# mLSTM sample states spread over the chunks of the last head, with their sum in another PSUM pool

## The chip, the cores and the metric

The kernel runs on one core of one Trainium2 chip. The metric is the device time of one execution in microseconds, the median of several runs.

## The reference

One layer of a hybrid decoder, over a prompt of 1,024 tokens and 8 samples of 4 tokens that share all weights: a SwiGLU feed-forward block, a mixer, a second SwiGLU block, and a gated per-layer embedding. The mixer projects the normalised tokens once and runs an S5 branch and an mLSTM branch. The change lies in the mLSTM branch:

```python
scores = jnp.einsum('bhtd,bhsd->bhts', qc, kc) * w
num = (jnp.einsum('bhts,bhsd->bhtd', scores, vc)
       + a[..., None] * jnp.einsum('bhtk,bhkv->bhtv', qc, C))
nq = jnp.sum(scores, axis=-1) + a * jnp.einsum('bhtk,bhk->bht', qc, n)
h = num / jnp.maximum(jnp.abs(nq), jnp.exp(-m_t))[..., None]
C_new = decay[..., None, None] * C + jnp.einsum('bhs,bhsk,bhsv->bhkv', wk, kc, vc)
n_new = decay[..., None] * n + jnp.einsum('bhs,bhsk->bhk', wk, kc)
```

The prompt starts from empty states and passes through 8 chunks of 128 tokens. Each of the 8 samples is one chunk of 4 tokens, and starts from given states: per sample and head a matrix C of 256 x 256 and a vector n of 256, which are read, used, updated and written. With 4 heads that is 32 matrices of 256 KB in and as many out. The output of both goes, after a norm by head and a gate `sigmoid(o)`, into the projection `w_m_up`.

## The kernel before

All 1,056 tokens are held with features on the partitions, in three column blocks of 384, 384 and 288 (`CH`). A product of the projections is made of three matmuls with operands split in a high and a low part (`mm3`, lines 115 to 117). The stages are in program order: feed-forward, gates, S5, conv and q/k, then for each head `head_proj` and `head_scan`, then `samples`, the output gate (`proj_tanh` with the name og), the S5 output (`s5_out`: glu, s5u), the join, feed-forward two, embedding, output.

The kernel is written in a framework that keeps a simulated timeline of the engines, and issues an instruction where that timeline has room for it. So the order on each engine isn't the program's: long products without dependences, such as og's 8 x 3 units of 24 matmuls, fill the places where TensorE would wait for a scan. The order is fixed when the kernel is built; on the chip each engine takes its instructions in that order and waits on semaphores. Buffers come from pools: 34 long tiles in SBUF ("slots"), which hold the q, k, v of a head, other tensors of the mixer, and the tiles of C; and two PSUM pools of four banks each, `pm` (tag "mm", for projections like og) and `pv` (tag "aux", for the scan and all small products).

`head_scan` (from line 1181) handles a head chunk by chunk: scores `s` (L1199), the transposed keys `kt` (L1202), weights from a row that is loaded for each chunk (L1196), the weighted scores split in `ps` (L99), their product with the values in `num`, the state's part (L1221), the state update `kv`, and `head_out`, whose transposes (`hT`, L1177) come one chunk later. After the last chunk the head's final state is stored (L1236, L1237).

`samples` is made of two parts. The first prepares: loads, transposes of n and of the keys (`nT` L1271, `ksT` L1278), the scores of all samples and heads at once (`sS`, L1286), from them `Pb` inside the tile `smA` (L1292), and K, V in split form. The second, the inner function `states`, is called after the scan of head 3. It makes the new n (`nn` L1317, added on VectorE at L1321 and L1322, transposed in `nnT` L1325 and stored), then one PSUM bank `snum` for the outputs of all samples: first the product with `Pb` (L1330), then for each of the 8 samples b and each pair of heads hh a tile `c0_b hh` of two matrices:

```python
for i in range(2):
    nc.sync.dma_start(ct[:, i, :, 0:256], ...)
v.tensor_copy(ct[:, :, :, 256:258], nz[...])
```

that is a load from SP (L1343) and a copy of the n columns on VectorE (L1344). Eight matmuls of 258 columns add the tile's part to `snum` (L1348); two matmuls a head make the key-value product `skv` (L1354), VectorE updates the matrices in place (L1356, 0.7 us each), and ScalarE's queue stores them (L1357). At the end `head_out` norms `snum`, transposes it (`hT_smp`) and stores it.

In the run order before, head 3's setup of the samples is called ahead of its scan, and `states()` behind it:

```python
if h == 3:
    states = self.samples()
self.head_scan(h, *qkv)
```

Of the kernel before, what the change touches and what calls it, by code (L numbers as in the profile page):

```python
# [7 lines left out]
F32 = mybir.dt.float32  # L8
# [7 lines left out]
P = 128  # L16
# [19 lines left out]
class Kernel:  # L36
# [1141 lines left out]
            return ps, self.hT[i % 2][:, :, :n]  # L1178
        return transposed

    def head_scan(self, h, q, k, vt):
        nc, v = self.nc, self.nc.vector
        gm = self.gain["g_mhead"]
        Cp = None

        def out(transposed, c):
            ps, hT = transposed()
            for kk in range(2):
                nc.scalar.activation(hT[:, kk], ps[:, kk], AF.Copy, scale=gm[:, 2 * h + kk:2 * h + kk + 1])
            nc.sync.dma_start(self.d_hm[2 * h:2 * h + 2, :, c * P:(c + 1) * P].rearrange("k p t -> p k t"), hT)  # L1190

        for c in range(8):
            nm, sl = f"{h}_{c}", slice(c * P, (c + 1) * P)
            z, wk, em = (self.cols[:, c, i, h:h + 1] for i in range(3))
            bc = self.bc[(8 * h + c) % 4]
            nc.sync.dma_start(bc.rearrange("p q t -> p (q t)"), self.d_row[h, c].rearrange("q t -> (q t)").unsqueeze(0).to_broadcast([P, 256]))  # L1196
            s = self.pv.tile([P, 512], F32, tag="aux", name=f"s{nm}")[:, :P]
            for kk in range(2):
                nc.tensor.matmul(s, k[kk][:, sl], q[kk][:, sl], start=kk == 0, stop=kk == 1)  # L1199
            kt = self.pv.tile([P, 512], F32, tag="aux", name=f"kt{nm}")[:, :256]  # L1200
            for kk in range(2):
                nc.tensor.transpose(kt[:, kk * P:(kk + 1) * P], k[kk][:, sl], self.ident)  # L1202
            kh, kl = (self.kw[:, c % 2, 256 * i:256 * i + 256] for i in range(2))
            nc.scalar.activation(kh, kt, AF.Copy, scale=wk)
            v.scalar_tensor_tensor(kl, kt, wk, kh.bitcast(F32), op0=ALU.mult, op1=ALU.subtract)
            vc = [x[:, c % 4] for x in vt[c // 4]]
            qp = self.pt.tile([P, 384], F32, tag="ss", name=f"qp{nm}")
            p, qa = qp[:, 256:], qp[:, :256].rearrange("p (k t) -> p k t", k=2)
            p2 = self.pt.tile([P, 384], F32R, tag="sq", name=f"ps{nm}")
            ph, pl = p2[:, :P], p2[:, P:2 * P]  # L1210
            v.tensor_tensor(p, bc[:, 0], self.mneg, ALU.add)
            nc.scalar.activation(p, p, AF.Exp, bias=z)
            v.scalar_tensor_tensor(p, s, 1.0 / 64, p, op0=ALU.mult, op1=ALU.mult)
            num = self.pv.tile([P, 512], F32, tag="aux", name=f"num{nm}")[:, :258]
            self.split(p, ph, pl)
            self.mm3(num, (ph, pl), *vc, True, c == 0)
            if c:
                for kk in range(2):
                    v.scalar_tensor_tensor(qa[:, kk], q[kk][:, sl], 1.0 / 32, bc[:, 1], op0=ALU.mult, op1=ALU.mult)
                for kk in range(2):  # L1220
                    nc.tensor.matmul(num, qa[:, kk], Cp[:, kk], start=False, stop=kk == 1)  # L1221
            Cn = self.C_[(8 * h + c) % 2]
            for kk in range(2):
                kv = self.pv.tile([P, 512], F32, tag="aux", name=f"kv{nm}_{kk}")[:, :258]
                ks = slice(kk * P, (kk + 1) * P)
                self.mm3(kv, (kh[:, ks], kl[:, ks]), *vc, True, True)
                if c:
                    v.scalar_tensor_tensor(Cn[:, kk], Cp[:, kk], self.decb[:, 16 * h + c:16 * h + c + 1], kv, op0=ALU.mult, op1=ALU.add)
                else:
                    v.tensor_copy(Cn[:, kk], kv)  # L1230
            Cp = Cn
            if c:
                out(transposed, c - 1)
            transposed = self.head_out(num, em, P, nm)
        out(transposed, 7)
        nc.sync.dma_start(self.outs[4][0, 0, h].rearrange("(k p) x -> p k x", p=P), Cp[:, :, 0:256])  # L1236
        nc.sync.dma_start(self.outs[5][0, 0, h].rearrange("(k p) -> p k", p=P), Cp[:, :, 256])  # L1237
# [12 lines left out]
    def samples(self):  # L1250
# [56 lines left out]
        def states():  # L1307
# [18 lines left out]
            no = self.pt.tile([P, 384], F32, tag="h", name="no")[:32, :256]  # L1326
            v.tensor_copy(no, ps)
            nc.sync.dma_start(self.outs[11][0].rearrange("b h k -> (b h) k"), no)
            num = self.pv.tile([P, 512], F32, tag="aux", name="snum")[:, :258]
            nc.tensor.matmul(num, Pb, self.vs, start=True, stop=False)  # L1330
            for b in range(8):
                bs = slice(4 * b, 4 * b + 4)
                qb = qm[b % 2]
                if b > 1:
                    v.memset(qb[:, :, 4 * b - 8:4 * b - 4], 0.0)
                v.tensor_tensor(qb[:, :, bs].rearrange("p (h k) t -> p h k t", k=2), self.qs[:, :, bs].rearrange("p (h k) t -> p h k t", k=2),
                                asb[:, :, bs].unsqueeze(2).to_broadcast([P, 4, 2, 4]), ALU.mult)
                km = kms[b % 2]
                v.tensor_scalar(km, K[:96, :NP].bitcast(F32).rearrange("p (h x) -> p h x", h=4), self.bmask[:96, b:b + 1], None, op0=ALU.mult)
                for hh in range(2):  # L1340
                    ct = self.px.tile([P, XW], F32, tag="s", name=f"c0_{b}{hh}")[:, :1032].rearrange("p (h k x) -> p h k x", h=2, k=2)
                    for i in range(2):
                        nc.sync.dma_start(ct[:, i, :, 0:256], a["state_mlstm_c"][0, b, 2 * hh + i].rearrange("(k p) x -> p k x", p=P))  # L1343
                    v.tensor_copy(ct[:, :, :, 256:258], nz[:, 4 * b + 2 * hh:4 * b + 2 * hh + 2])  # L1344
                    for kk in range(2):
                        for i in range(2):
                            h = 2 * hh + i
                            nc.tensor.matmul(num[32 * h:32 * h + 32], qb[:, 2 * h + kk], ct[:, i, kk],  # L1348
                                             start=False, stop=b == 7 and kk == 1)
                    for i in range(2):  # L1350
                        h = 2 * hh + i
                        kv = self.pv.tile([P, 512], F32, tag="aux", name=f"skv{b}_{h}").rearrange("p (k x) -> p k x", k=2)
                        for kk in range(2):
                            nc.tensor.matmul(kv[:, kk], km[:, h, kk * P:(kk + 1) * P], V[:96, 256 * h:256 * h + 256], start=True, stop=True)  # L1354
                        cc = ct[:, i, :, 0:256]
                        v.scalar_tensor_tensor(cc, cc, self.decb[:, 16 * h + 8 + b:16 * h + 9 + b], kv, op0=ALU.mult, op1=ALU.add)  # L1356
                        nc.scalar.dma_start(self.outs[10][0, b, h].rearrange("(k p) x -> p k x", p=P), cc)  # L1357
# [167 lines left out]
    def run(self):  # L1525
# [22 lines left out]
        self.scan_setup()  # L1548
        for h in range(4):
            qkv = self.head_proj(xm, sm, w_in, h)  # L1550
            if h == 3:
                states = self.samples()
            self.head_scan(h, *qkv)
        states()
        self.proj_tanh(xm, rb, w_in[:, 3584:4608], self.d_to, "og")
        self.s5_out_load()
        self.s5_out()
# [37 lines left out]
```

## Time and profile before

| | |
|---|---|
| median of 3 runs | 2270.72 us (2268.5 to 2270.73) |
| profiled execution, its own time | 2271.5 us |
| its span, first to last instruction | 2269.8 us |
| mean granted clock of TensorE | 0.994 of full speed |
| TensorE (PE) busy | 2232.9 us, 98%, 15,712 matmuls |
| VectorE (DVE) busy | 1379.9 us, 61% |
| ScalarE (ACT), GpSimd (POOL) busy | 821.7 us, 36%; 501.7 us, 22% |
| DMA | 240.47 MB, 106 GB/s mean |
| chain that ended last | PE 88%, DVE 5%, DMA 4% |

The chain that ended last is followed back from the last instruction to what released each piece; 88% of it is TensorE. A timeline row gives start, duration and, in brackets, the idle time before it with what ended that. Durations of matmuls that follow one another overlap, so their cost is the distance from start to start. A window row gives for a stretch the busy time of each engine and the granted clock as a share of 2.4 GHz.

### The profile page before, as it was taken

Reading aid. Unit: us, or ns where it says so; the run is one execution under the profiler, and the core shown is the slowest. Engines: PE = TensorE matmul, PEld = TensorE weight load, DVE = VectorE, ACT = ScalarE, POOL = GpSimd, SP = SyncE. Lnnn points to the kernel's source line nnn. Section 1 sums busy time; section 2 is a strip of 40 time slices with the busy share of each in tenths; the row PEclk is TensorE's granted clock in tenths of the full one; section 3 lists DMA queues with packets and bytes.
Section 4 is the critical chain, followed back from the end, with each engine's and each line's share of the span. In section 5 each row is a group of like instructions: output and inputs, shape, how many; then the busy total and the mean of one; then the engine's idle time right before and its main releaser. Section 6 shows DMA issues by size and latency. Waiting matters only on the chain.

```text
span 2269.8 us, 39784 instructions
## 1 busy us (share of the span) xinstructions
PE 2232.9 (98%) x15712; PEld 2194.9 (97%) x15712; DVE 1379.9 (61%) x3190; ACT 821.7 (36%) x1552; POOL 501.7 (22%) x528
## 2 busy tenths in 40 slices
PE   7999999999999999999999999999999999999999
PEld 6999999999999999999999889999999999999998
DVE  5854556336768857769686477545665556523754
ACT  6433333114334433444344233224433333311543
POOL 1476763000001000000000000003477666000000
PEclk9999999999999999999999999999999999999999
DMA  5223237223344542222223587342122233711201
GB/s 189 78 68 94 76 95 246 74 69 111 88 126 132 139 122 64 55 64 54 61 63 113 154 275 262 121 152 76 62 80 74 75 95 95 262 64 56 60 20 77
DMA packets 286146, 240.47 MB, mean 106 GB/s; under 512 B 28748, under 2 KB 263212, under 8 KB 285960
## 3 DMA queue, kind: packets, MB, share of 16 engines
q1 hardware_dynamic: 266720, 216.34, 31.0%
q10 hardware_dynamic: 19240, 21.59, 2.8%
q8 instruction: 123, 2.02, 0.4%
q14 instruction: 63, 0.52, 0.1%
HBM read 168.04 MB, written 67.35 MB: 104 GB/s over the span
## 4 chain that ended last, share of the span: by engine, by line
PE 88%; DVE 5%; DMA 4%; issue 1%; SPq 1%; ACT 1%; POOL 0%; ACTq 0%; DVEq 0%
PE mm_qk L115 3%; PE mm_qk L116 3%; PE mm_qk L117 3%; PE mm_f1d L117 2%; PE mm_f1d L115 2%; PE mm_f1d L116 2%; PE mm_f2d L115 2%; PE mm_f2d L116 2%; PE mm_f2d L117 2%; PE mma_f2u L191 2%; PE mmd_f2u L191 2%; PE mmc_f2u L191 2%; PE mmc_f2g L191 2%; PE mmd_f2g L191 2%; PE mma_f2g L191 2%; PE mmc_f1g L191 2%
## 5 line engine op out<-in xcount | busy, mean ns | idle before, releaser
L115 PE MATMUL mm_qk<-n2h,wh_qk 128*128 128x384 f32 (+1 forms) x384 | 126.0, 328 | 0.0
L116 PE MATMUL mm_qk<-n2l,wh_qk 128*128 128x384 f32 (+1 forms) x384 | 125.4, 327 | 0.0
L117 PE MATMUL mm_qk<-n2h,wl_qk 128*128 128x384 f32 (+1 forms) x384 | 125.2, 326 | 0.0
L115 PE MATMUL mm_f1d<-f1hh,wh_f1d 128*128 128x384 f32 (+1 forms) x384 | 122.8, 324 | 1.8 <-DVE x_f L565 1.8
L115 PE MATMUL mm_f2d<-f2hh,wh_f2d 128*128 128x384 f32 (+1 forms) x384 | 123.5, 326 | 1.0 <-ACT f2hh L98 1.0
L117 PE MATMUL mm_f2d<-f2hh,wl_f2d 128*128 128x384 f32 (+1 forms) x384 | 123.7, 323 | 0.0
L116 PE MATMUL mm_f1d<-f1hl,wh_f1d 128*128 128x384 f32 (+1 forms) x384 | 123.7, 323 | 0.0
L117 PE MATMUL mm_f1d<-f1hh,wl_f1d 128*128 128x384 f32 (+1 forms) x384 | 123.7, 323 | 0.0
L116 PE MATMUL mm_f2d<-f2hl,wh_f2d 128*128 128x384 f32 (+1 forms) x384 | 123.6, 323 | 0.0
L1166 POOL TENSOR_TENSOR cy<-cs,mhalf 128x1 f32<-128x1 f32 x32 | 20.2, 632 | 442.2 <-DVE cs L1165 419.2
L429 POOL TENSOR_TENSOR rc_n<-nv_n,mhalf 128x3 f32<-128x3 f32 x9 | 8.9, 984 | 444.0 <-DVE nv_n L425 407.6
L565 DVE SCALAR_TENSOR_TENSOR x_f<-mm_f2d,x_f 128x384 f32<-128x384 f32 (+1 forms) x72 | 37.2, 521 | 94.9 <-PE mm_f2d L117 92.8
L565 DVE SCALAR_TENSOR_TENSOR x_f<-mm_f1d,x_f 128x384 f32<-128x384 f32 (+1 forms) x72 | 36.9, 521 | 93.3 <-PE mm_f1d L117 90.6
L1108 DVE SCALAR_TENSOR_TENSOR cv<-raw,vecs,cv 128x384 f32<-128x384 f32 (+1 forms) x144 | 84.8, 589 | 7.3 <-ACT cv L1106 6.0
L115 PEld LDWEIGHTS mm_f1d<-f1hh,wh_f1d 128*128 128x128 f32 x384 | 71.9, 188 | 2.6 <-DVE x_f L565 2.5
L115 PEld LDWEIGHTS mm_f2d<-f2hh,wh_f2d 128*128 128x128 f32 x384 | 71.9, 188 | 1.8 <-ACT f2hh L98 1.2
L116 PEld LDWEIGHTS mm_qk<-n2l,wh_qk 128*128 128x128 f32 x384 | 72.3, 188 | 0.1
L115 PEld LDWEIGHTS mm_qk<-n2h,wh_qk 128*128 128x128 f32 x384 | 72.3, 188 | 0.0
L117 PEld LDWEIGHTS mm_qk<-n2h,wl_qk 128*128 128x128 f32 x384 | 72.2, 188 | 0.1
L116 PEld LDWEIGHTS mm_f1d<-f1hl,wh_f1d 128*128 128x128 f32 x384 | 72.2, 188 | 0.0
L117 PEld LDWEIGHTS mm_f2d<-f2hh,wl_f2d 128*128 128x128 f32 x384 | 72.1, 188 | 0.1
L116 PEld LDWEIGHTS mm_f2d<-f2hl,wh_f2d 128*128 128x128 f32 x384 | 72.1, 188 | 0.0
(761 smaller groups left out, 7370.7 us busy)
## 6 DMA issues: line engine op xcount, KB each, us to landing
d_f1h<-f1h SPq DMA_DIRECT2D x16, 528.0 KB
f1hl<-d_f1h SPq DMA_DIRECT2D x16, 528.0 KB
x_f<-d_xs SPq DMA_DIRECT2D x16, 528.0 KB
d_f2h<-f2h SPq DMA_DIRECT2D x16, 528.0 KB
f2hl<-d_f2h SPq DMA_DIRECT2D x16, 528.0 KB
wr_qk<-in_w_in_dram SPq DMA_DIRECT2D x16, 512.0 KB
c<-in_state_mlstm_c_dram SPq DMA_DIRECT2D x32, 256.0 KB
out_dram<-c ACTq DMA_DIRECT2D x32, 256.0 KB
```

Source lines behind the costliest of these rows:

```text
L115: mm(ps, wh, xh, start=start, stop=False)
L116: mm(ps, wh, xl, start=False, stop=False)
L117: mm(ps, wl, xh, start=False, stop=stop)
L191: nc.tensor.matmul(ps, w[:, wq, i], f[q][:, xq, cs], start=start and i == j == 0, stop=i == n - 1 and j == 2, skip_group_check=not start)
L429: nc.gpsimd.tensor_tensor(r, ms, self.mhalf[:, :nt], ALU.pow)
L565: v.scalar_tensor_tensor(xs, ps, 0.5, xs, op0=ALU.mult, op1=ALU.add)
L1108: v.scalar_tensor_tensor(acc, raw[:, o + i:o + i + wd], self.cw[:, i, T:T + 1], acc, op0=ALU.mult, op1=ALU.add)
L1166: nc.gpsimd.tensor_tensor(y, ss, self.mhalf[:n, 0:1], ALU.pow)
```

## The change

`head_scan` takes a function `then` and calls it after each chunk. `states` becomes a generator: a `yield` stands ahead of each sample of its loop. The run order scans heads 0 to 2 as before; then it calls the setup and makes the generator, and scans head 3 with `then` drawing one step. So after chunk 0 the part up to the first product into `snum` is written, after chunk c the sample c - 1, and after the scan sample 7 with the closing part. And `snum` takes its bank from `pm`, where og's units have theirs.

```diff
-    def head_scan(self, h, q, k, vt):
+    def head_scan(self, h, q, k, vt, then=lambda: None):
...
             transposed = self.head_out(num, em, P, nm)
+            then()
         out(transposed, 7)
...
-            num = self.pv.tile([P, 512], F32, tag="aux", name="snum")[:, :258]
+            num = self.pm.tile([P, 512], F32, tag="mm", name="snum")[:, :258]
             nc.tensor.matmul(num, Pb, self.vs, start=True, stop=False)
             for b in range(8):
+                yield
                 bs = slice(4 * b, 4 * b + 4)
...
         for h in range(4):
             qkv = self.head_proj(xm, sm, w_in, h)
-            if h == 3:
-                states = self.samples()
-            self.head_scan(h, *qkv)
-        states()
+            if h < 3:
+                self.head_scan(h, *qkv)
+        states = self.samples()()
+        self.head_scan(3, *qkv, lambda: next(states))
+        for _ in states:
+            pass
```

Lines of `samples` move down by one or two: the first product into `snum` is L1331, the load L1345, the copy L1346, the update L1358.

On TensorE, at the start of head 3's scan, where the setup's scores `sS` have just been made, the order changes as follows (`s_0` and `kt_0` are chunk 0's scores and transposed keys, `mm_og_0` is og's first unit, `smA` holds Pb):

```order
-L1286 MATMUL sS<-mlE 32x32 x8
+L1272 MATMUL nT<-ident,nin 128x32 x2
+L1279 MATMUL ksT_13462<-ident,mlE 32x128 x4
+L1279 MATMUL ksT_13463<-ident,mlE 32x128 x4
+L1287 MATMUL sS<-mlE 32x32 x8
+L1199 MATMUL s_0_13529<-q_0_12714,k_0_12716 128x128
+L1199 MATMUL s_0_13529<-q_1_12715,k_1_12717 128x128
+L1202 MATMUL kt_0_13532<-ident,k_0_12716 128x128
+L1202 MATMUL kt_0_13532<-ident,k_1_12717 128x128
+L1331 MATMUL snum<-mlE,smA 128x258
 L115 MATMUL mm_og_0_14343<-n2h_5775,wh_og_14339 128x384
```

Before, og's first product stood right behind `sS`; now chunk 0's `s` and `kt` and the first product into `snum` stand between them.

On VectorE, at chunk 3 of head 3, the order before was (`qp_3` are the weighted scores, `ps_3` their split, `kw` the weighted keys, `cd_2` a column of chunk 2's `head_out`):

```order
L1213 SCALAR_TENSOR_TENSOR qp_3_13695<-s_3_13687,qp_3_13695 128x128
L1165 TENSOR_SCALAR cs_2_13672<-cs_2_13672 128x1
L99 TENSOR_TENSOR ps_3_13696<-qp_3_13695,ps_3_13696 128x128
L1167 TENSOR_TENSOR cd_2_13670<-cy_2_13673 128x1
L1168 TENSOR_TENSOR cd_2_13670<-cd_2_13670,cs_2_13672 128x1
L1205 SCALAR_TENSOR_TENSOR kw<-kt_3_13690,cols,kw 128x256
```

At the same place the order of the change is:

```order
L1358 SCALAR_TENSOR_TENSOR c_11_13775<-c_11_13775,decb,skv_3_13788 128x2x256
L1341 TENSOR_SCALAR sm_13496<-smK,bmask 96x1024
L1213 SCALAR_TENSOR_TENSOR qp_3_13802<-s_3_13794,qp_3_13802 128x128
L1346 COPY c_20_13852<-smA 128x4x2
L1205 SCALAR_TENSOR_TENSOR kw<-kt_3_13797,cols,kw 128x256
L99 TENSOR_TENSOR ps_3_13803<-qp_3_13802,ps_3_13803 128x128
```

The update of tile c_11 and the copy into tile c_20 now stand among chunk 3's work, the copy ahead of its `kw` and `ps`. The tile c_20 takes the buffer of tile c_10.

## Rows read from the trace of the kernel before

**Rows 1.** Windows of 10 us: busy of PE, PEld, DVE, ACT, POOL (count), PEclk, DMA share, GB/s.
```profile
1290.00:1300.00 10.00, 6.74 (x48) 6.45 (x47) 1.29 (x5) 2.21 (x4) 0.00 (x0) 0.96 0.81 140
...
1350.00:1360.00 10.00, 9.26 (x61) 8.91 (x60) 10.00 (x20) 4.22 (x10) 0.00 (x0) 1.00 0.62 201
```

**Rows 2.** Waits of TensorE, 1195 to 1365: us in total, times, longest us.
```profile
PE nnT L1325 <- DVE smA L1322: 3.3, 1, 3.3
PE hT_smp L1177 <- DVE mlC L1172: 0.7, 1, 0.7
```

**Rows 3.** Timeline of TensorE around nnT: start us, us, engine, line, operation.
```profile
1296.39 0.34 PE L117 MATMUL mm_og<-n2h,wl_og 128*128 128x384 f32 x1
1299.99 0.58 PE L1325 MATMUL nnT<-ident,smA 128*32 128x128 f32 x2 [3.26 <-DVE smA L1322]
```

**Rows 4.** Windows behind three waits of TensorE, columns as in rows 1.
```profile
1299.20:1306.00 6.80, 6.01 (x32) 2.98 (x34) 3.60 (x9) 0.45 (x1) 0.00 (x0) 0.50 0.41 126
...
657.50:667.70 10.20, 8.45 (x41) 8.05 (x42) 5.25 (x19) 1.50 (x2) 0.48 (x1) 0.50 0.41 95
...
561.00:567.00 6.00, 6.00 (x37) 6.00 (x37) 6.00 (x16) 4.53 (x9) 0.00 (x0) 1.00 0.96 311
```

**Rows 5.** Chain that ended last, ahead of nnT: start us, us, what.
```profile
1288.33 0.56 SPq L1237
1288.94 10.56 DMA c<-in_state_mlstm_c_dram
1299.59 0.13 DVE c L1344
```

**Rows 6.** Chain that ended last: og, and a c tile's round trip.
```profile
1277.62 0.13 PE mm_og L116
...
1282.36 5.50 DMA c<-in_state_mlstm_c_dram
...
1307.11 0.37 PE mm_og L115
1307.48 0.18 PE mm_og L116
1307.66 0.23 PE skv L1354 x2
...
1308.07 0.17 PE mm_og L115
...
1312.27 0.76 DVE c L1356
1313.06 4.30 DMA out_dram<-c
1317.43 0.37 SPq L1343
1317.85 3.92 DMA c<-in_state_mlstm_c_dram
```

**Rows 7.** Timeline of VectorE: Pb (smA, L1292) with its neighbour, and an og evacuation.
```profile
1205.67 1.22 DVE L99 TENSOR_TENSOR wl_og<-wr_og,wh_og 128x1024 fp32r<-128x1024 f32 x1
1206.81 0.78 DVE L1292 SCALAR_TENSOR_TENSOR smA<-sS,smA 32x32 f32<-32x32 f32 x4
...
1291.90 0.56 DVE L628 TENSOR_TENSOR t_og<-mm_og,rb_n 128x384 f32<-128x384 f32 x1 [1.53 <-PE mm_og L117]
```

**Rows 8.** Timeline of TensorE, start of head 3's scan.
```profile
1203.83 0.44 PE L115 MATMUL mm_og<-n2h,wh_og 128*128 128x384 f32 x1
...
1207.60 0.61 PE L1199 MATMUL s<-q,k 128*128 128x128 f32 x4
...
1208.18 0.42 PE L115 MATMUL mm_og<-n2h,wh_og 128*128 128x384 f32 x1
```

**Rows 9.** Timeline of TensorE: two other waits.
```profile
560.76 0.40 PE L115 MATMUL mm_f1d<-f1hh,wh_f1d 128*128 128x288 f32 x1 [1.50 <-DVE x_f L565]
...
659.25 0.48 PE L787 MATMUL h0T<-ident,s5w 128*128 128x128 f32 x1 [3.82 <-DMA s5w<-in_state_s_re_dram]
```

## The prediction

> **What bounds the kernel now.** I read the table of busy times first: TensorE is busy for nearly the whole span, so time is won or lost only where it stands still or runs at its lower clock. The 10 us windows around the change come second. There TensorE is full, except that it does 6.74 us in 1290 to 1300 and 9.26 us in 1350 to 1360 [rows 1]. The list of its waits over 1195 to 1365 names two: 3.3 us for nnT, 0.7 us for hT_smp [rows 2]. In the timeline the last og product ends at 1296.73 and nnT starts at 1299.99 [rows 3]. The granted clock then stands at 0.50, which is 1.2 GHz, from 1299.20 to 1306.00, with TensorE busy 6.01 us of it [rows 4].
>
> Why nnT waits is read from the chain that ended last. VectorE takes its work in order, and the add into smA that nnT needs stands behind a copy into a c tile whose load took 10.56 us; that load was issued right behind the scan's last store (L1237) [rows 5]. So a state load that is late for a later tile holds back the first tile's sum.
>
> **What the old place costs.** The wait is 3.26 us. Work of 6.01 us at half clock would be 3.0 us at full clock: 3.0 lost. The wait before hT_smp is 0.74. Together 7.0 us can be won, no more, since TensorE has no other wait there.
>
> **The change, part by part.**
>
> *Instructions.* Matmuls, loads, updates and stores of the samples stay the same in number and shape. TensorE's work does not change, only its neighbours do. Counted along the two orders from sS to the end of glu, TensorE changes between og-like and full fp32 products 87 times before and 79 times now. The first og product after snum products takes 0.37, a later one 0.17 [rows 6]; eight changes fewer, half of them into og, are 4 x 0.20 = **-0.8**.
>
> *Removed.* nn, its add and nnT now stand in the second chunk's og products, ahead of any late load; the scan's last store now stands behind all c loads on SP. The 3.26, the 3.0 of clock, and the 0.74 (snum ends well before glu) go: **-7.0**.
>
> *Added at the head.* snum's first product moves to just behind sS and chunk 0's s and kt, ahead of every og product. It needs Pb, the masked score block. VectorE finishes Pb only at 1206.81 + 0.78 = 1207.59, since the og weight split (1.22 us) stands ahead of it [rows 7], and its order up to Pb is unchanged. TensorE follows sS with og at 1203.83; s and kt take 1208.18 - 1207.60 = 0.58 [rows 8]. So TensorE reaches snum at 1203.83 + 0.58 = 1204.41 and waits 1207.59 - 1204.41 = **+3.2**. Behind snum in TensorE's order stands all of og, which hid Pb before; now that cover is gone. The bounds are 0, if VectorE gets Pb done sooner, and 3.3.
>
> *Clock after it.* No row shows this wait, so I take its neighbours. The 3.26 wait was followed by 6.80 us at 0.50, a 3.82 wait by 10.20 us at 0.50 (8.45 busy) and a 1.50 wait by full clock [rows 3, 4, 9]. 3.2 lies beside 3.26, so the drop is likely: **+3.0**, bounds 0 and 4.2 (half of 8.45).
>
> *The c tiles.* Before, the 16 tiles of c were spread over some eleven buffers and came at the end. Now, beside the live tiles of head 3, two buffers are free, a third after chunk 3. So each of the tiles from c_10 to c_41 waits for its predecessor's round trip: update 0.76, store 4.30, SP 0.37, load 3.92, which with what lies between is 1317.85 + 3.92 - 1312.27 = 9.5; with a load of 5.50 it is 11.1 [rows 6]. What TensorE has to do between, counted along its order (og at 0.175, the mean of its 0.17 and 0.18, or 0.13; two skv 0.23 [rows 6]), is 10.2 us ahead of c_10, 9.4 ahead of c_11, 9.5 ahead of c_21, 12 to 13 from c_40 on. For c_20 it is worst: VectorE's copy into c_20 stands ahead of chunk 3's kw and ps, so the chunk's num waits for the load too. From tile 10's last product to that num lie 37 og of 384 columns (6.5), 10 of 288 (1.3), four skv (0.46), s and kt (0.6): 8.9. c_31 (9.7) and c_41 (10.4) stand so as well. Against 9.5 the stalls are 0.6 and a little, against 11.1 they run to 2.2, 1.7, 1.6, 1.4, 0.9 and 0.7, sum 8.5; but one stall lengthens the gap of the next, so I take half of it as the upper end, then add a clock drop: 0 to 7. Value: **+2.0**, nearer the first end, since transfers are now spread over the whole scan, where the rows come from a crowded stretch.
>
> *og's bank.* snum holds one of og's four banks for the whole scan. A unit of 24 products takes 24 x 0.175 = 4.2 us, its evacuation on VectorE 0.56 [rows 7]; with three banks two units (8.4 us) hide it: **0**. If VectorE were held by a c copy for over 8 us the bank would matter; this is inside the c tiles' upper end.
>
> *Tail.* The y5 load of the last quarter now waits for a buffer of chunk 7; a late one costs at most a load, 5.5 [rows 6]. I take **0**, since og still follows.
>
> *Sum.* -0.8 - 7.0 + 3.2 + 3.0 + 2.0 = +0.4. The profiled execution is 2271.5, its span 2269.8; the sum makes it 2271.9. The median is 2270.72, so on its scale **2271.1 us**: no change. One stall at the scan's end is traded for one at its head.
>
> **A rule against the change.** The rows show a repeated two-buffer round trip with 0.6 to 2.2 us between need and arrival [rows 6]. The Trainium skill, "Perfetto Trace Analysis", section "Optimization Strategy", says that the same gap repeating on the engine that should be saturated can mean too little SBUF or PSUM for the next tile. By it the gap would return with each batch; that is rival B. The Trainium skill, "TensorE: Matmul & The Clock Gate", section "HAM oscillation", describes a loop whose wait for data re-throttles the clock in every round, so that the work behind starts slow; by it rival B would pay the clock each time. Here the 1.50 wait kept full clock [rows 4, 9], which speaks against that for short stalls.
>
> **The rivals.**
> *A, faster.* The head's wait leaves the clock at full and the c tiles come in time: -0.8 - 7.0 + 3.2 = -4.6, so 2266.1. For it: 1.50 left the clock alone. Against: 3.26 and 3.82 did not. Should Pb also come 1.2 earlier (the og split issued behind it), 2264.9. Chance 0.24.
> *B, slower.* The two-buffer round trip sets the pace of batches 1 to 4. It decides when store plus load take over about 10 us in the new place. With loads of 5.50 the stalls are 4.3, and if two of them run together past 3 us the clock adds 3.0: +7.3 in place of +2.0, so 2276.4; with a second such drop 2279.4. For it: the 10.56 us load [rows 5]. Against: that load shared the queues with the scatter store, now moved. Chance 0.26.
> *C, nothing new.* Of the forecast's terms only sizes vary. 0.50. That the change does nothing is excluded by the order: nnT and snum do move.
>
> **How the numbers follow.** About 0.2% (4.5 us) is what a measurement of this kernel can tell from no change: faster lies below 2266.2, slower above 2275.3. A falls just below the first, B above the second. C's own range is 2267 to 2275: the c tiles 0 to 5, the clock 2 to 4. The range of 8 in 10 takes in most of A and half of B: 2265.3 to 2277.5. Chances: faster 0.23, same 0.52, slower 0.25.
>
> **What would show it.** Right: in TensorE's waits, nnT and hT_smp gone; snum's first product waiting some 3 us for smA from VectorE at about 1204; the granted clock at 0.5 for some microseconds behind it and at 1.0 around 1300; waits of 0 to 2 us ahead of num of chunks 3 to 5 or snum, released by VectorE's c copy or the c load. Wrong: no wait at snum's first product, or og running ahead of it (A and less); full clock after the wait (A); stalls that repeat with each batch beyond 2 us (B); a wait of og for its bank; glu waiting for y5.

## The result, and the profile after

The change is slower: 2285.62 us median of 4 runs (2283.55 to 2286.87), against 2270.72 before. The ratio is 1.0065 [1.0053, 1.0077]. Forecast were 2271.1 us and no change, with a range up to 2277.5; the result lies 8 us above it. The profiled execution of the change has a span of 2285.1, which is 15.3 more than before's 2269.8.

Windows of before, cut at three places in TensorE's order: the end of `sS`, the last of glu and cvT (the transposes of the conv branch), the end of the up projection `mm_mu`. Columns as in [rows 1]:

```profile
1203.90:1375.70 171.80, 167.80 (x1106) 154.19 (x1106) 111.46 (x320) 68.18 (x148) 4.86 (x9) 0.98 0.62 195
1375.70:1514.60 138.90, 138.90 (x864) 138.90 (x863) 82.00 (x154) 34.26 (x61) 0.00 (x0) 1.00 0.48 163
```

The same two stages after:

```profile
1205.50:1382.40 176.90, 171.62 (x1104) 155.49 (x1105) 108.55 (x315) 69.33 (x148) 4.84 (x9) 0.99 0.61 181
1382.40:1529.80 147.40, 141.87 (x866) 140.59 (x865) 84.43 (x159) 34.10 (x61) 0.00 (x0) 0.99 0.48 163
```

The first stage, head 3's scan with the samples, takes 5.1 us longer. The second, s5u and the join, takes 8.5 us longer, though the change names nothing in it: there TensorE had no idle time before, and has 5.5 now. The start took 1.6 more; nothing in it is changed, and the end of `sS` lay between 1201.9 and 1207.4 over the kernels of this study, but for one that moves work from ahead of it to behind it. So totals are read beside their stages below.

TensorE's waits of 1195 to 1480 after, columns as in [rows 2]:

```profile
PE mm_s5u L115 <- DVE g L1410: 2.8, 2, 1.8
PE mm_mu L115 <- DVE g L1410: 2.6, 1, 2.6
PE snum L1331 <- DVE smA L1293: 2.3, 1, 2.3
PE skv L1356 <- ACT mlC L1189: 1.9, 1, 1.9
PE hT L1177 <- DVE mlC L1172: 0.7, 1, 0.7
PE s L1199 <- DVE smA L1274: 0.2, 1, 0.2
```

nnT and hT_smp [rows 2] are gone, as forecast. The wait at snum's first product is there, as forecast. The others are new. TensorE's timeline at the head, columns as in [rows 3], where [rows 8] had og right behind `sS`:

```profile
1205.12 0.35 PE L1287 MATMUL sS<-mlE 128*32 128x32 f32 x16
1205.64 0.71 PE L1199 MATMUL s<-q,k 128*128 128x128 f32 x4 [0.17 <-DVE smA L1274]
1206.48 0.41 PE L1202 MATMUL kt<-ident,k 128*128 128x128 f32 x2
1209.22 0.70 PE L1331 MATMUL snum<-mlE,smA 128*128 128x258 f32 x2 [2.33 <-DVE smA L1293]
```

Windows after: the two spells at half clock (the second follows the 1.83 us wait before s5u), the place of nnT in [rows 1], and what follows the waits for skv and mu:

```profile
1210.23:1213.65 3.42, 3.42 (x13) 3.42 (x12) 3.24 (x11) 2.62 (x8) 0.00 (x0) 0.50 1.10 341
1418.45:1421.86 3.41, 3.41 (x13) 3.41 (x12) 1.90 (x6) 0.99 (x2) 0.00 (x0) 0.50 1.02 406
1290.00:1300.00 10.00, 10.00 (x65) 9.10 (x64) 3.81 (x18) 2.45 (x8) 0.00 (x0) 1.00 0.73 244
...
1351.97:1360.00 8.03, 8.03 (x53) 8.00 (x54) 4.54 (x10) 2.11 (x3) 0.00 (x0) 1.00 0.86 276
...
1440.40:1448.00 7.60, 7.60 (x49) 7.60 (x50) 6.36 (x15) 1.28 (x3) 0.00 (x0) 1.00 0.61 213
```

Work that runs at half clock for 3.41 us loses 1.7. Before, TensorE worked for 6.01 us at half clock [rows 4], so 3.0 were lost; the rest of that spell is idle time. From this each stage can be split:

| | idle | lost at half clock | the rest | stage |
|---|---|---|---|---|
| scan and samples, before | 4.0 | 3.0 | 164.8 | 171.8 |
| scan and samples, after | 5.3 | 1.7 | 169.9 | 176.9 |
| s5u and join, before | 0 | 0 | 138.9 | 138.9 |
| s5u and join, after | 5.5 | 1.7 | 140.2 | 147.4 |

In the scan the rest, that is the work itself at full clock, grows by 5.1, with the same matmuls. Summed from the start of each instruction to that of the next, the products into snum grow from 13.8 to 16.9, hT and og by 1.0 each, kt and num by 0.4 each, and skv falls by 0.9. The reason for snum is seen in pieces of TensorE's timeline, before:

```profile
1317.02 1.09 PE L1348 MATMUL snum<-c,mlD 128*32 128x258 f32 x16
1318.05 0.50 PE L1354 MATMUL skv<-smV,sm 96*128 96x256 f32 x2
1318.47 1.07 PE L1348 MATMUL snum<-c,smA 128*32 128x258 f32 x8
1319.47 0.51 PE L1354 MATMUL skv<-smV,sm 96*128 96x256 f32 x2
```

and after:

```profile
1219.58 1.06 PE L1350 MATMUL snum<-c,mlD 128*32 128x258 f32 x8
1220.58 0.44 PE L117 MATMUL mm_og<-n2h,wl_og 128*128 128x384 f32 x1
...
1247.23 1.06 PE L1350 MATMUL snum<-c,smA 128*32 128x258 f32 x6
1248.22 0.50 PE L1356 MATMUL skv<-smV,sm 96*128 96x256 f32 x2
1248.64 0.62 PE L1350 MATMUL snum<-c,smA 128*32 128x258 f32 x2
1249.20 0.44 PE L116 MATMUL mm_og<-n2l,wh_og 128*128 128x384 f32 x1
```

Eight records (one tile) take 1.00 from start to the next start; sixteen (two tiles) take 1.03. Each product writes 32 of the 128 output rows of the bank (`128*32`), one such strip per head, and products for different strips run side by side where they are adjacent. A tile that another product breaks into 6 and 2 records takes 0.99 + 0.56. Before, the 130 records of snum stood in 13 stretches of up to 24; now they stand in 19, of which 12 are single tiles and six belong to tiles broken in two.

At the end of the scan the chain that ended last, columns as in [rows 5], runs through the head's last store:

```profile
1334.69 0.22 SPq L1237
...
1334.96 12.66 DMA out_dram<-mlA
...
1347.70 0.54 ACT y5h L98
...
1349.92 1.16 ACT y5h L98 x3
...
1351.79 0.14 ACT mlC L1189
...
1351.97 0.51 PE skv L1356 x2
```

Before, a c load behind that store was late [rows 5]. Now no c load stands behind it, but a part of y5h on ScalarE can start only when it has landed, 12.66 us after its issue (ScalarE stands idle for the last 2.13 of them), and mlC and skv stand behind y5h.

### The profile page after: what moved, and what is told of

Its sections match the earlier page's. It is cut to its first block, busy times and chain, and to the rows that moved or that the text cites. A ratio compares the mean times of both kernels' runs of the same rounds, so it can differ in the third digit from the quotient of the medians.

```text
span 2285.1 us, 39761 instructions
## 1 busy us (share of the span) xinstructions
PE 2240.9 (98%) x15712; PEld 2199.5 (96%) x15712; DVE 1378.9 (60%) x3190; ACT 822.6 (36%) x1552; POOL 500.5 (22%) x528
## 4 chain that ended last, share of the span: by engine, by line
PE 88%; DVE 6%; DMA 3%; ACT 1%; issue 1%; SPq 1%; POOL 0%; POOLq 0%; ACTq 0%; DVEq 0%
PE mm_qk L115 3%; PE mm_qk L116 3%; PE mm_qk L117 3%; PE mm_f1d L117 2%; PE mm_f1d L115 2%; PE mm_f1d L116 2%; PE mm_f2d L116 2%; PE mm_f2d L115 2%; PE mm_f2d L117 2%; PE mma_f2u L191 2%; PE mmd_f2u L191 2%; PE mmc_f2u L191 2%; PE mmc_f2g L191 2%; PE mmd_f2g L191 2%; PE mmc_f1g L191 2%; PE mmc_f1u L191 2%
```

## The experiments

**What the two halves cost.** One kernel has the new bank alone, in the kernel before:

```diff
-            num = self.pv.tile([P, 512], F32, tag="aux", name="snum")[:, :258]
+            num = self.pm.tile([P, 512], F32, tag="mm", name="snum")[:, :258]
```

> The kernel before with snum's bank from og's pool, and nothing spread. Theory P: snum's first product again stands ahead of og's first, though the states are written behind the whole scan, so the head's wait and its clock drop come (+4), and the late nnT wait stays as before; by theory J the part of s5u that is turned round here (5_0, 6_0, 5_1 to the end, half as many places as in the change) costs about half of 8.3: 2279 (2275 to 2281). Rival F (spreading is what costs): the bank alone does nothing, 2270.7 (2268 to 2273).

Measured: 2283.2 us, 1.0057 [1.0042, 1.0072]. Its waits of TensorE, 1195 to 1515 (the first two rows):

```profile
PE snum L1348 <- DVE c L1344: 3.3, 1, 3.3
PE snum L1330 <- DVE smA L1292: 2.3, 1, 2.3
```

The bank alone, with the states still written behind the scan, brings the head's wait of 2.3 and costs nearly as much as the whole change. In all seven kernels with this bank in which og was left alone, og's first unit stands behind snum's first product. That product was drawn ahead of og even here, where it is written after the scan. The records of snum stand in 24 stretches and take 19.2 us; the join, at 139.2, is as before. The other kernel has the spreading alone, the same line turned back in the changed kernel:

> The changed kernel with snum's bank from the scan's pool again; the states are spread as in the change. Theory P: og's first unit follows sS again, as before the change, and the head's wait goes: about -4; the order of s5u is still turned round (3_0, 4_0, 3_1 and so on), so theory J keeps its 8.3: 2281.6 (2279 to 2284). Rival B (banks): with snum in it, the scan's pool has three banks left for s, kt, num, kv, hT and skv, and TensorE waits for them in each chunk, 8 chunks by 0.5 to 1 us: 2286 to 2290.

Measured: 2292.04 us, 1.0096 [1.0081, 1.0111]: the worst of all. glu waits 10.6 us for y5h, and 13.65 us at half clock follow. The bank and the spreading both lose, and the losses do not add.

**The wait at the head.** og's first tile is written ahead of head 3's scan, so that its units get their banks before snum:

```diff
         states = self.samples()()
...
+        self.proj_tanh(xm, rb, w_og, self.d_to, "og", (0,))
         self.head_scan(3, *qkv, lambda: next(states))
...
```

> The changed kernel, with the first of og's eight tiles written ahead of the scan of head 3, so that its three units take their banks before snum does. Theory P (the pool hands out banks in program order): snum's place in og's pool holds every og product behind snum's first product, and so behind Pb; with one tile ahead, 72 og products stand between sS and snum, the wait of 2.3 us and the half clock behind it (3.4 us, 1.7 lost) go: 2281.6 (2280 to 2283). Rival: the wait comes back at snum or nnT, or the clock falls at another place: 2285 (2284 to 2287).

Measured: 2281.59 us, 1.005 [1.0033, 1.0067]. 72 og products now run ahead of snum; the head's wait of 2.3 and the drop behind it, worth 1.7, are gone. The median falls by 4.0, which fits, but not by that alone. The profiled runs lie 6.3 apart: the start is 1.8 shorter, the scan stage only 1.9, the join 2.8. In the scan stage other waits came in: glu waits 3.1 for y5h, and snum waits three times, 2.4 in all, for the copy into a c tile. A spell of 3.41 us at half clock comes at its end.

**The join.** In the changed kernel the order of the s5u units on TensorE is turned round in places (unit 4_0 ahead of 3_1). Here all s5u units are held in program order:

```diff
...
-                ps = self.unit(w, y2, j, f"s5u{m}_{j}", m % 2, aux=m % 2 == 1)
+                ps = self.unit(w, y2, j, f"s5u{m}_{j}", m % 2, aux=m % 2 == 1, pin=m + j > 0)
```

> The changed kernel, with the units of the S5 up projection (s5u) kept on TensorE in the order in which the program writes them; nothing else is changed. Theory J (the join's order): from the end of glu and cvT to the end of mu the changed kernel takes 8.3 us more than before (147.4 against 139.1), because its order puts the first unit of each next tile ahead of the last two of the one before, which holds each pair of weights and each PSUM bank one unit longer; with the order restored the waits at s5u and mu (2.8 and 2.6 us) go, and the time is 2277.5 (2276 to 2280). Rival S (the stream): the loads of g, hm and to come late whatever the order, since each group of them stands behind a weight load on SP that waits for a buffer; then the waits only move to other units and the time stays at 2285 (2283 to 2287). Rival F (all of the loss is in the scan): also 2285.

Measured: 2285.92 us, 1.0067 [1.0052, 1.0082]. The wait of mu is gone and the join falls from 147.4 to 142.9; but the scan stage takes 178.6 (6.83 us at half clock in two spells, skv waits 2.5), so the total stays. Both edits together:

> The kernel of e2 (one og tile written ahead of snum) with the s5u units kept in program order as in e1. In e2's trace the join still waits 2.6 us ahead of the first mu product and 0.8 at s5u, with a clock drop behind (3.4 us at half, 1.7 lost). Theory J' (order and late loads each cost a part of the join: in e1 the order alone took its stage from 147.4 to 142.9): without the turned order e2's join of 144.6 falls to 139.5 to 141: 2277.5 (2276 to 2279). Rival S (loads of to and hm late, 3 us behind the end of glu in e2 against 8 us ahead of it before): the wait moves to other units and the time stays at 2281.6 (2280 to 2283).

Measured: 2279.83 us (2275.62 to 2281.45), 1.0029 [1.0017, 1.004]. The join is 141.2. But in the scan stage glu waits 6.1 us for y5h, and 10.24 us at half clock follow. Its chain that ended last:

```profile
1340.69 14.13 DMA out_dram<-mlA
...
1354.93 0.13 ACT y5h L98
```

The store is here again, now before glu.

The conv branch's output (`conv_out`, which shares row buffers with the join's loads) moved from behind glu to before head 3's v projection:

```diff
-        self.conv_out()
         for m in range(KT):
...
+        if h == 3:
+            self.conv_out()
         vt = [[self.ph.tile([P, NT], F32R, tag="s", name=f"vh{h}_{i}")
```

> The changed kernel with the output of the conv state (cvT, cvo) written ahead of head 3's value projection instead of behind glu, so that the two pr buffers which the join's to tiles use are not held by it. Theory S (the pr buffers): to is loaded some 20 us sooner, the s5u and mu waits (5.5 us and the 1.7 of clock) go; the order on TensorE also changes at the head, where value products now fill the wait for Pb (2.3 and 1.7 gone as in e2): 2273.5 (2271 to 2277). Rival J (the order of s5u is what costs): it comes out in program order here by itself, so the join falls as well; but then e5 shows it too. Rival F (both are symptoms of a scan that ends late): 2281 to 2285.

Measured: 2280.4 us, 1.0036 [1.0023, 1.0049]. The join is 138.9, with no idle time, as before the change. But at the head kt waits 2.7 us for cvo, and v3t 2.3, with 6.83 us at half clock. The s5u units come out in program order in this kernel, so it does not tell the row buffers from that order. Another kernel only gives the conv output's tiles other buffers (`self.pr`, the rows, to `self.px`, the slots):

> The changed kernel, with the conv state's output tiles (cvo) from the pool of long tiles in place of the pool pr; the scan's order and the samples stay as in the change, and SP issues the first to load some places earlier. Theory S (pr): with to loaded earlier the join's waits fall (5.5 us and 1.7 of clock at most): 2279 (2277 to 2283). Rival J (the order of s5u alone; it stays turned round here): 2285.6 (2283 to 2287).

Measured: 2285.59 us, 1.0049 [1.0035, 1.0063]. s5u's waits fall from 2.8 to 0.7, mu's 2.6 stays; the join is 144.5.

**The stall that the change aimed at.** Only the new n (`nn`, nnT and its store) is given out ahead of head 3's scan; all else is as before:

```diff
+            yield
             num = self.pv.tile([P, 512], F32, tag="aux", name="snum")[:, :258]
...
+                states = self.samples()()
+                next(states)
             self.head_scan(h, *qkv)
-        states()
+        for _ in states:
+            pass
```

> The kernel before, with only the new n (nn, its add, nnT, its store) given out ahead of head 3's scan; snum, in the scan's pool, and the states stay behind it. This is the gain that the change aimed at, alone. Theory: the nnT wait of 3.26 and its clock loss of 3.0 go, nothing else moves much: 2264.5 (2262.5 to 2267). Rival C (the late c tile): the copy into the late tile still stands ahead on VectorE, so the wait comes back at snum, as in e4, where snum waits 3.3 us for the c copy: 2270.5 (2268.5 to 2273).

Measured: 2279.65 us, 1.0033 [1.002, 1.0046]. nnT waits no more, but skv does:

```profile
PE skv L1355 <- ACT mlC L1189: 5.6, 1, 5.6
PE skv L1355 <- DVE c L1357: 1.4, 2, 0.8
PE mm_glu L115 <- ACT y5h L98: 1.2, 1, 1.2
```

with two spells of 6.83 us at half clock, and its chain has the same late load:

```profile
1298.91 10.72 DMA c<-in_state_mlstm_c_dram
...
1311.58 0.37 ACT mlC L1189
...
1311.99 0.80 PE skv L1355 x2
```

So nnT was not the cause, only the first to wait. The suspect is the store that stands before the late load in [rows 5]: head 3's final n (L1237), 256 single elements of 4 bytes, each to an address of its own. In the next kernel, the one before with this edit, the n of all heads are collected, transposed on TensorE, and stored at once as 8 rows of 128 elements:

```diff
-        nc.sync.dma_start(self.outs[5][0, 0, h].rearrange("(k p) -> p k", p=P), Cp[:, :, 256])
...
+        v.tensor_copy(self.nfin[:, 2 * h:2 * h + 2], Cp[:, :, 256])
+        if h == 3:
...
+            nc.tensor.transpose(ps, self.nfin, self.ident)
...
+            nc.sync.dma_start(self.outs[5][0, 0].rearrange("h (k p) -> (h k) p", p=P), o)
```

> The kernel before, with the four heads' final n (L1237) gathered in one tile, transposed once and stored as eight rows, in place of four stores of single elements. Theory N (the scattered store): the last of these stores stood right ahead of the c load that took 10.56 us; without it the c tile comes some 5 us sooner, the nnT wait (3.26) and its clock loss (3.0) go or shrink: 2265 (2263 to 2267.5) against 2271 for the kernel before. Rival: the load was slow for its neighbours on the queues, not for the store; the wait stays: 2271 (2269 to 2273).

Measured: **2262.76 us** (2261.94 to 2265.77), **0.9961 [0.9948, 0.9973]**. TensorE's waits, 1195 to 1515, and the windows from before the stall to the end of the join:

```profile
PE hT_smp L1177 <- DVE mlC L1172: 0.7, 1, 0.7
```
```profile
1290.00:1367.90 77.90, 77.16 (x536) 66.34 (x535) 56.64 (x123) 33.87 (x61) 0.54 (x1) 1.00 0.79 256
1367.90:1506.80 138.90, 138.90 (x864) 138.90 (x864) 82.70 (x156) 34.45 (x61) 0.00 (x0) 1.00 0.49 163
```

The wait and the half clock are gone, in the old order: this is the version that beats both kernels. That all four stores changed leaves open which one counted, so one more kernel is the one before without the store of head 3's n (that row of the output is left out):

> The kernel before without the store of head 3's final n (L1237, one store of 256 single elements); that output row is left out, all other stores and the stores of heads 0 to 2 stay. Theory N: this one store is the whole of the late c load, so the time is e9's: 2263 (2261.5 to 2266). Rival: part of e9's gain came from the stores of heads 0 to 2 or from the order that the new rows gave: 2266 to 2271.

Measured: 2266.7 us (2262.91 to 2266.94), 0.9974 [0.9962, 0.9985]. The scan stage is 165.6, that of the rows 165.7, before 171.8. The total is 3.9 above that of the rows, within the rival's 2266 to 2271, but 3.2 of it lie ahead of the scan, in the start. VectorE's copy into the late c tile, before and in this kernel:

```profile
1299.59 0.17 DVE L1344 COPY c<-smA 128x8 f32<-128x8 f32 x1 [7.13 <-DMA d_to<-t_og]
...
1296.37 0.17 DVE L1345 COPY c<-smA 128x8 f32<-128x8 f32 x1 [2.44 <-DMA c<-in_state_mlstm_c_dram]
```

The copy's wait falls from 7.13 to 2.44 (in the first row the profile names another DMA that landed at that moment; the chain [rows 5] names the load). On TensorE the stall is gone: the one store is the cause.

**The change with the store mended.** The same edit in the changed kernel:

> The changed kernel with the final n stored as rows, nothing else. If the scattered store costs the changed kernel only what stands behind it (skv's wait of 1.9 for ScalarE and some lateness of y5), 2282.5 (2280 to 2285); then the spreading costs about 20 us against e9 (2262.8), where the stall that it aims at is absent. Rival: most of the change's loss is this store as well, as e5 against e10 (6.6 us) would let one think, or more: 2276 to 2279.

Measured: 2279.56 us, 1.0034 [1.0022, 1.0047]. The wait of skv is gone, so it did hang on the store; hT still waits 0.4. With the store mended the change is still 16.8 us behind the best kernel (by medians): its scan stage is 174.0 against 165.7, its join 145.7 against 138.9. With og's tile ahead and s5u in order as well:

> The kernel of e5 (states spread, one og tile ahead of snum, s5u in order), with the final n stored as rows as in e9. In e5's chain the same store takes 14.13 us and ends right ahead of ScalarE's y5h, for which glu waits 6.1 us, with 10.24 us at half clock behind (5.1 lost). Theory N: these 11 us go: 2269 (2267 to 2273). Rival: y5h waits for the y5 loads and glu still stands; 2278 to 2280.

Measured: 2273.19 us (2272.29 to 2277.48), 1.001 [1.0001, 1.0019]. glu's wait falls from 6.1 to 0.5, with no drop of the clock in either stage; s5u waits 2.7 and hT 1.7. No tile of snum is broken here: its records stand in 13 stretches again and take 14.4. Adding the conv output's other buffers:

> The kernel of e10 (states spread, one og tile ahead of snum, s5u in order, n as rows) with cvo's tiles from the long pool as in e11. What is left of the join in e10 (142.4 against 138.9, s5u waits of 2.7) is by theory S the pr buffers: 2270 (2268.5 to 2272). Rival: the to and hm loads stay late for the weight load ahead of them on SP: 2273 (2272 to 2275). In both cases it stays above e9: what the spreading itself costs (hT, snum and og beside one another) is the rest.

Measured: 2276.03 us (2272.12 to 2277.14), 1.0013 [1.0005, 1.0022]; the join is 145.2, not shorter than 142.4. The waits of s5u for g fall from 2.7 to 1.4, but its first units now wait 1.7 for y6h, with 3.41 us at half clock behind. So the part of the shared row buffers is not shown in this pair.

**The groups of snum.** In the kernel before, the products of both tiles of a sample are put side by side:

```diff
...
+                for kk in range(2):
+                    for h in range(4):
+                        mm = nc.tensor.matmul(num[32 * h:32 * h + 32], qb[:, 2 * h + kk], cts[h // 2][:, h % 2, kk],
...
```

> The kernel before, with both tiles of a sample brought together: the eight matmuls of all four heads' column groups into snum stand next to each other for each sample, and nothing stands between them. Theory G (groups): four heads run beside one another in TensorE's column groups, two heads take as long as four (1.07 us for a group of 8, 1.09 for a group of 16 in the trace of before); snum's 13.8 us (clock taken out) fall to about 8 x 1.1 + 1 = 9.8: 2266.7 (2264 to 2269), if the late nnT wait and its clock stay. Rival: waiting for both tiles costs what the groups give: 2270.5 (2268.5 to 2273).

Measured: 2271.82 us, 1.0002 [0.9993, 1.0012]. snum falls from 13.8 to 11.5, as side by side it should; but skv now waits 0.8 and glu 1.1, and the wait at nnT, 3.4, stays. Together with the n in rows:

> The kernel before, with e7's eight neighbours in snum and e9's rows together. In e7 the snum time fell by 2.3 us and waits of 1.1 at glu (for y5h) and 0.8 at skv came in. Theory N with G: the nnT wait goes and the snum gain shows: 2263 (2260 to 2266). Rival: as e9's rival, 2271; or the gain of the groups is eaten by the wait for both tiles, 2265 as e9.

Measured: 2264.91 us, 0.9966 [0.9954, 0.9979], no better than rows alone.

**The join's loads.** In the changed kernel the loads of the join stand on SP in another order: w_m_up's weights come 14 to 15 us apart, not 11 to 12, and the heads' tiles behind them. Part of the chain that ended last after, before the 1.83 us wait of s5u:

```profile
1397.76 8.24 DMA to<-d_to
...
1406.09 1.39 DVE hm L1425 x3
...
1410.01 1.23 DVE wl_mu L99
1411.25 0.38 SPq L106
...
1411.73 5.37 DMA g<-d_t
1417.13 0.56 DVE g L1410
```

A late `to` holds `hm` on VectorE; `wl_mu` stands behind it; SP's next weight load waits for that; and the load of g stands behind it on SP. Here the weights are put back in their old place in SP's order, first in the changed kernel:

```diff
...
+            with self.tc.issue_after(after.ins):
+                nc.sync.dma_start(raw, src.rearrange("(k p) m -> p k m", p=P))
...
```

> The changed kernel, with the join's weight loads put back on SP to where they stood before: the loads of g, hm and to stand ahead of them again (in the change SP's fourth mu weight load waits 13.8 us behind the end of glu for its raw buffer, with g, hm and to of the next two tiles queued behind it; before, those were issued at 2.7). s5u stays turned round. Theory Q (head of SP's queue): the join's waits (5.5 us) and clock drop (1.7) go: its stage falls from 147.4 to 139 to 141, the time to 2278.5 (2276.5 to 2280.5). Rival J (the order of s5u is needed too): 144 and 2282 to 2284.

Measured: 2285.59 us, 1.006 [1.0048, 1.0073]. s5u's waits fall from 2.8 to 1.0, mu's 2.6 stays; the join is 144.8. And in the kernel with the rows, og ahead and s5u in order:

> The kernel of e10 (states spread, one og tile ahead of snum, s5u in order, n as rows) with the same order of loads on SP. Theory Q: e10's join of 142.4 falls to 139 to 139.5: 2270 (2268.5 to 2271.5); every loss that was found in the change is then mended, and what is left against e9 (2262.8) is the spreading's own: waits of 2.6 us in the scan, hT, snum and og beside one another 1.5 us, and noise. Rival: the join stays at 142: 2273 (2272 to 2275).

Measured: 2274.45 us (2271.14 to 2276.46), 1.0009 [1.0, 1.0018]; the join is 141.5 against 142.4 without it, and s5u still waits 2.0. Three causes have a part in the join. Put back one at a time in the changed kernel, the order of the s5u units gives 4.5 of the 8.5 us, the row buffers 2.9 and SP's order 2.6; 1.7 of the 4.5 is the clock, which fell in the other two joins and not in that one. They are not independent: with the bank alone the s5u units are turned round in places too, and the join takes 139.2. With the orders of s5u and of SP put back 2.6 remain. What holds these is not settled.

## Why the prediction was wrong

Against the terms of its sum, in order:

- **Removed, -7.0: right.** The 3.26 and 0.74 are gone, and the clock is 1.00 from 1290 to 1300. With the store as rows the scan stage fell by 6.1, where the wait and the clock make 6.3.
- **Head, +3.2: right in kind, sized 0.9 too high.** Pb was as late as forecast, but `s` and `kt` took 1206.89 - 1205.64 = 1.25, not 0.58. The 0.58 was read from a place where og stands on both sides and kt overlaps with it; before, kt is the row between the last two of [rows 8]:

```profile
1208.04 0.38 PE L1202 MATMUL kt<-ident,k 128*128 128x128 f32 x2
```

There `s` took 0.44 to the start of kt and kt 0.14 to that of og; here `s` took 0.84, and kt 0.41 to its end, since nothing follows it. Why `s` took longer is not shown. The wait was 2.33, and 0.17 stood before `s`.
- **Clock behind it, +3.0: right in kind, 1.7.** The spell was 3.41 us, not 6.80.
- **c tiles, +2.0: about 0.** VectorE's list of waits for 1195 to 1382 has the round trip:

```profile
DVE c L1346 <- DMA c<-in_state_mlstm_c_dram: 14.6, 10, 3.8
```

It waited ten times, yet TensorE waited for no c in this stage, so rival B did not come. The rule of the Trainium skill ("Perfetto Trace Analysis", section "Optimization Strategy") is on gaps that repeat on the engine that should be saturated; here they repeated on VectorE. But B's mechanism is there: in four of the five kernels with og's tile ahead snum does wait for the copy into a c tile, 1.0 to 2.4 us in all. In the first of them (2281.59 us) the chain ahead of such a wait of 1.2 us is the round trip:

```profile
1242.10 3.10 DMA out_dram<-c
...
1246.14 5.23 DMA c<-in_state_mlstm_c_dram
```

- **Alternations, -0.8: wrong.** The prediction counted changes between og and the samples' products, and said "TensorE's work does not change, only its neighbours do". Its own kernels had the counter-evidence in the timeline: 16 records of snum in 1.03, 8 in 1.00. By neighbours alone the work grew by 5.1, 3.1 of it in snum.
- **og's bank, 0: right that og never waits for one, wrong in what the bank does.** It decides whether og or snum comes first, and how snum's products lie: alone it costs 12.7 us (the medians of that comparison: 2283.2 against 2270.48).
- **Tail, 0: the failed step.** "I take 0, since og still follows." The store of 256 single elements lasts as long as before; moved behind the c loads, it meets y5h, and skv pays 1.9. hT pays 0.7, of which 0.4 stays without the store. And the sum ended at glu. The join behind it, which the change does not touch, was not in it at all: +8.5, the largest term.

Together: -7.0 + 2.5 (head) + 1.7 + 2.6 (skv and hT) + 5.1 + 8.5 + 1.6 (start) = 15.0, where the span grew by 15.3. The low end of rival C's range, 2267, is a slip: by its own terms it is 2268.1. The rivals missed too: A kept the head's wait without its clock, B had the wrong place; the chance for slower, 0.25, stood on B.

Under the aim of the change lies another step. The prediction took the stall to be a matter of order: a tile's sum stood behind a late load. It noted that this load was issued right behind the scan's last store, and used the store only as an argument against B. The load was late because of that store; with the store as rows the old order has no stall to move. That makes the change needless; what made it slow are the head, the neighbours and the join.

## What to carry to other kernels

Ask first why a load is late, and only then what stands behind it: moving the consumer took the stall from nnT to skv (5.6 us), mending one 1 KB store took it away. Where a scheduler sets the order, the account has to run on until the two orders are the same again, to the end of the join here, and a pool's bank is an edit of the order. When work is spread over a longer stretch, count how its products lie side by side, not their number alone.

## What the runs showed of the hardware that was not expected

- A store of 256 single elements, 1.0 KB, is on the chain for 12.66 us in the change and for 10.99 to 14.13 in six other kernels as itself, and a c load right behind it for 10.56, 10.72 and 11.60, where other c loads of the same size took 3.92 and 5.50 [rows 6].
- The length of a wait does not tell what the clock does: behind 1.83 us (s5u) it stood at 0.50 for 3.41 us, behind 1.93 (skv) and 2.64 (mu) at 1.00. With og's tile ahead the same wait of 2.64 before mu was followed by 3.41 us at 0.50. The prediction took the 1.50 us wait without a drop [rows 9] for a sign that short waits are spared. The Trainium skill, "TensorE: Matmul & The Clock Gate", section "HAM oscillation", describes waits that re-throttle the clock; here some did and some did not.
- Products that write different strips of 32 output rows cost almost nothing beside each other where they are adjacent: sixteen records in 1.03 us, eight in 1.00. Eight records broken into 6 and 2 take 0.99 + 0.56.
